# Order of the second mixers: products written between the steps of a recurrence

## The chip, the cores and the metric

The kernel runs on one core of a Trainium2 chip. The metric is the time of one execution on the device in microseconds; lower is better. Five engines work side by side, each on a queue of its own in a fixed order: TensorE (PE in the profile; its weight loads are PEld), VectorE (DVE), ScalarE (ACT), GpSimd (POOL) and SyncE (SP), which issues the transfers.

## The reference, cut to what matters

Two networks of two layers each work on 512 positions of 1024 channels, the second on the output of the first. The change touches the mixer of the second network, which runs three mixers on slices of one projection and joins them:

```python
def hybrid_mixer(h, positions, w_in, ...):
    proj = h @ w_in
    aq, ak, av, bq, bf, bv, bg, cqkv, cg, cb, ca = jnp.split(proj, split_at, axis=-1)
    # A: attention in a window of 128
    aq = partial_rope(rmsnorm_2(aq, q_norm), positions)
    ak = partial_rope(rmsnorm_2(ak, k_norm), positions)
    out_a = sliding_window_attention(aq, ak, av, sinks)
    # B: gated linear recurrence (HGRN2)
    log_f = jnp.logaddexp(jnp.log(lb), jnp.log1p(-lb) + jax.nn.log_sigmoid(bf))
    o_b = hgrn2_chunked(bq, log_f, bv)
    out_b = rmsnorm_2(o_b, hgrn_norm) * jax.nn.silu(bg)
    # C: gated delta rule, on convolved queries, keys and values
    cq, ck, cv = jnp.split(jax.nn.silu(causal_depthwise_conv(cqkv, conv_w)), ...)
    o_c = gated_delta_chunked(l2norm(cq), l2norm(ck), cv, beta, g)
    out_c = rmsnorm_2(o_c, gdn_norm) * jax.nn.silu(cg)
    return jnp.concatenate([out_a, out_b, out_c], axis=-1) @ w_out
```

## The kernel before, in words

Activations are held channel by channel: eight tiles of 128 channels x 512 positions. Every projection is a product in three parts: weights and activations are each split into a rounded half and the rest, and three matmuls (high x high, high x low, low x high) add up in PSUM. `load` (line 391) fetches a weight tile on SyncE, ScalarE rounds it (L381) and VectorE takes the rest (L382).

There are two kinds of product. A feature-major one (`lin_f_steps`) gives a tile of 128 output channels x 512 positions from 24 matmuls (lines L406, L407, L408 of `mm3`); its result goes to a function `ev`. A token-major one (`lin_t_steps`) gives four blocks of 128 positions; it yields after each eighth of its inner dimension, that is after 12 matmuls (L475, L476, L477), and evacuates all four blocks at its end. Both take their PSUM banks under the tag `mm`, which has four.

`second_mixer` runs in this order. Four feature-major products (w[0:4]) give the recurrence's gates and queries. One token-major product (`win2_t0`, 512 wide) gives its values and output gate, and the first two steps of the recurrence `hgrn` are taken between its last steps. Then the rest of `hgrn` is written out: two pairs of heads woven together, 10 steps each. In each of eight levels of a pair GpSimd takes a difference (L1260), ScalarE two exponentials (L1261, L1262), VectorE scales queries and keys (L1264, L1265), TensorE multiplies them (L1273), and VectorE merges the result into an accumulator (L1277, L1279). The two last steps of a pair combine the chunks (L1288 to L1312) and apply the values (L1330). The recurrence's PSUM tiles go under the tag `mx`, four banks, two per step.

Behind the recurrence stand a token-major product of 392 columns (`win2_t1`: the attention's values, the delta rule's gate `cg` and its two small gates), the gain of `cg` on GpSimd (L1751), and five feature-major products (w[10:15]): four tiles of the attention's queries and one of its keys. Their evacuation `ev` scales them (L1721), squares them (L663) and sums the squares per head by small matmuls into the tile `st` (L1724). The attention `swa` then rotates the five tiles on VectorE (L1084 to L1087) and normalises, until it says "ready". Six more feature-major products follow (w[4:10]), each with a convolution on VectorE (L832 to L844). Last, the attention and the delta rule `gdn` are woven step by step.

The written order is not the order in the queues. A planner in the framework takes it as a priority: it goes through the program with estimated durations and gives each engine the first ready instruction in the written order, and it assigns the buffers of each tag on the way. The queues are fixed before the run.

Of the kernel before, what the change touches and what calls it, by code (L numbers as in the profile page):

```python
# [249 lines left out]
class Net:  # L250
# [1456 lines left out]
    def second_mixer(self, x, l):  # L1707
        nc, V, G = self.nc, self.nc.vector, self.nc.gpsimd
        keep = {}

        def ev(o, ps):
            if 4 <= o < 10:
                keep[o] = L.conv(ps, self.vec("conv_w2", l)[:, 4 * (o - 4):4 * (o - 4) + 4], 3, None)
                return
            t = keep[o] = L.t(name="u")
            if o < 4:
                nc.scalar.copy(t, ps)
                return
            if o == 10:
                keep["st"] = self.ps("mx")  # L1720
            nc.scalar.activation(out=t, in_=ps, func=AF.Copy, scale=self.vec("q_norm" if o < 14 else "k_norm", l))  # L1721
            sq, i = self.square(ps), o - 10
            for b in range(NB):
                nc.tensor.matmul(keep["st"][:, 10 * b + 2 * i:10 * b + 2 * i + 2], sq[:, b * P:(b + 1) * P], self.bd64[:, 0:65:64],  # L1724
                                 start=True, stop=True)

        bv, bg, cg = (self.big((P, NB, 256), name=n) for n in ("bv", "bg", "cg"))
        L = self.using("l")
        av = L.t((P, NB, P), name="av")
        ba = self.small((P, NB, 8), "gba", 2)  # L1730

        def gate(t, ps):

            nc.scalar.activation(out=t, in_=ps, func=AF.Tanh, scale=0.5)
            V.scalar_tensor_tensor(t, t, 1.0, ps, op0=ALU.add, op1=ALU.mult)

        def evt0(b, ps):
            nc.scalar.copy(bv[:, b, :], ps[:, 0:256])
            gate(bg[:, b, :], ps[:, 256:512])

        def evt1(b, ps):
            nc.scalar.copy(av[:, b, :], ps[:, 0:128])
            gate(cg[:, b, :], ps[:, 128:384])
            V.tensor_copy(ba[:, b, :], ps[:, 384:392])

        w = self.tiled("win2_f", l, KD)
        y_a, y_c, last = [], [], []

        def gains(t, n):
            t4 = t.rearrange("p a (b c) -> p (a b) c", b=4)  # L1750
            G.tensor_tensor(t4, t4, self.row(n, l).unsqueeze(1).to_broadcast([P, 16, 64]), op=ALU.mult)  # L1751

        self.lin_f(w[0:4], x, ev, wide=4)
        gh = self.using("m", "mx").hgrn([keep[2], keep[3]], [keep[0], keep[1]], bv, bg, l, last)
        for n, _ in enumerate(self.lin_t_steps(self.d["win2_t0"][l], x, 512, evt0)):
            if n + 1 in (7, 8):
                next(gh)
        for n, _ in enumerate(gh):
            if n == 2:
                gains(bg, "hgrn_norm")  # L1760
        self.lin_t(self.d["win2_t1"][l], x, 392, evt1)
        gains(cg, "gdn_norm")
        self.lin_f(w[10:15], x, lambda o, ps: ev(o + 10, ps))
        ga = self.using("l", "mx").swa([keep[o] for o in range(10, 14)], keep[14], keep["st"], av, l, self.tab2, y_a)
        while next(ga) != "ready":
            pass
        y_b = last[0]()
        self.lin_f(w[4:10], x, lambda o, ps: ev(o + 4, ps))
        gc = self.using("m", "mm").gdn([keep[o] for o in range(4, 10)], cg, ba, l, y_c)
        drain(weave(gc, ga))  # L1770
        return y_a + y_b + y_c
# [49 lines left out]
def weave(*gens):  # L1821

    gens = list(gens)
    while gens:
        for g in list(gens):
            try:
                new = next(g)
            except StopIteration:
                gens.remove(g)
            else:  # L1830
                if new is not None:
                    gens.append(new)
                yield


def drain(gen):
    for _ in gen:
        pass
# [25 lines left out]
```

## Time and profile before

| | us |
|---|---|
| median of 3 runs | 3588.67 |
| lowest and highest | 3587.6, 3591.35 |
| the profiled execution | 3586.55 |
| its span, first to last instruction | 3584.7 |
| TensorE busy in the span | 3484.3 |
| VectorE busy | 1989.1 |
| ScalarE busy | 1364.5 |

The second network's mixers lie between 2100 and 2500 us (layer 0) and between 2840 and 3240 us (layer 1) of the span. A row of the timeline gives start, duration, engine, line, operation, the tiles written and read, their shapes and a count; in brackets stands how long the engine had been idle and what released it. A matmul's duration holds its run through the array, so neighbours overlap: a slot is the distance of two starts. PEclk is the granted TensorE clock as a share of 2.4 GHz.

### The profile page before, as it was taken

The numbers are of one execution on the slowest core, as the hardware profiler recorded it, in microseconds if no ns is written. First come the engines' busy times: TensorE is split into PE (matmuls) and PEld (weight loads), VectorE is DVE, ScalarE is ACT, GpSimd is POOL, SyncE is SP. The second block draws the span as 40 slices with busy tenths as digits, with TensorE's granted clock in tenths as the row PEclk, the third lists the DMA queues.
The fourth block names the chain that finished last, engine by engine and source line by source line (L and its number), as shares of the span: only waits on it lengthen the run. The fifth ranks groups of instructions, "written<-read, shape, count | busy, mean of one in ns | idle before, by whom it ended". The sixth has DMA issues, their size and how long they took to land.

```text
span 3584.7 us, 44503 instructions
## 1 busy us (share of the span) xinstructions
PE 3484.3 (97%) x17694; PEld 2901.8 (81%) x17694; DVE 1989.1 (55%) x3074; ACT 1364.5 (38%) x2231; POOL 140.5 (4%) x130
## 2 busy tenths in 40 slices
PE   9999999999999999999999998899999989999999
PEld 7888777888888888777888887788888877888887
DVE  6555665554665555674556577756333475654333
ACT  4223454323333223463223364354222453543221
POOL 0000000000000000000000003100000021000000
PEclk9999999999999999999999999899999999999999
DMA  5444212444334443202444321102333222022332
GB/s 167 141 135 129 84 32 68 142 145 128 127 100 142 146 138 100 91 15 95 146 148 137 94 77 54 62 7 75 108 98 101 78 71 68 1 71 90 100 99 83
DMA packets 114272, 349.06 MB, mean 97 GB/s; under 512 B 11536, under 2 KB 27920, under 8 KB 114064
## 3 DMA queue, kind: packets, MB, share of 16 engines
q1 hardware_dynamic: 114064, 346.21, 30.8%
q8 instruction: 140, 2.29, 0.3%
q14 instruction: 68, 0.56, 0.0%
HBM read 339.87 MB, written 2.10 MB: 95 GB/s over the span
## 4 chain that ended last, share of the span: by engine, by line
PE 87%; DVE 6%; issue 3%; ACT 2%; POOL 1%; DMA 1%; SPq 0%; POOLq 0%; DVEq 0%; ACTq 0%
PE mm L406 24%; PE mm L408 24%; PE mm L407 24%; PE mm L1481 1%; PE mm L1476 1%; PE mm L476 1%; PE mm L477 1%; PE mm L475 1%; PE mx L968 1%; DVE hacc L1279 1%; DVE wlo L382 1%; PE mm L809 1%; PE mx L948 1%; ACT sc L1138 1%; PE mx L1121 1%
## 5 line engine op out<-in xcount | busy, mean ns | idle before, releaser
L381 ACT CAST whi<-wraw 128x1024 fp32r<-128x1024 f32 (+3 forms) x540 | 553.4, 1029 | 1553.6 <-PE mm L407 1271.7
L406 PE MATMUL mm<-xh,whi 128*128 128x512 f32 (+1 forms) x2784 | 1053.3, 380 | 9.7 <-ACT whi L381 6.4
L407 PE MATMUL mm<-xl,whi 128*128 128x512 f32 (+1 forms) x2784 | 1055.8, 380 | 1.6 <-DVE xl L588 1.4
L408 PE MATMUL mm<-xh,wlo 128*128 128x512 f32 (+1 forms) x2784 | 1055.8, 380 | 0.3 <-DVE wlo L382 0.3
L382 DVE TENSOR_TENSOR wlo<-wraw,whi 128x1024 fp32r<-128x1024 f32 (+3 forms) x540 | 643.7, 1194 | 274.9 <-ACT whi L381 234.3
L406 PEld LDWEIGHTS mm<-xh,whi 128*128 128x128 f32 x2784 | 522.4, 189 | 107.8 <-ACT whi L381 6.4
L407 PEld LDWEIGHTS mm<-xl,whi 128*128 128x128 f32 x2784 | 524.9, 189 | 100.3 <-DVE xl L588 2.5
L408 PEld LDWEIGHTS mm<-xh,wlo 128*128 128x128 f32 x2784 | 524.8, 189 | 100.4 <-DVE wlo L382 3.1
L408 PE MATMUL mm<-hi,wlo 128*128 128x512 f32 (+1 forms) x1390 | 532.2, 383 | 2.1 <-DVE wlo L382 2.1
L406 PE MATMUL mm<-hi,whi 128*128 128x512 f32 (+1 forms) x1390 | 532.5, 384 | 0.2
L407 PE MATMUL mm<-lo,whi 128*128 128x512 f32 (+1 forms) x1390 | 531.8, 383 | 0.0
L408 PEld LDWEIGHTS mm<-hi,wlo 128*128 128x128 f32 x1390 | 261.3, 188 | 54.2 <-DVE wlo L382 4.2
L406 PEld LDWEIGHTS mm<-hi,whi 128*128 128x128 f32 x1390 | 261.1, 188 | 51.4 <-ACT hi L399 1.1
L407 PEld LDWEIGHTS mm<-lo,whi 128*128 128x128 f32 x1390 | 261.3, 188 | 50.3
L658 DVE SCALAR_TENSOR_TENSOR h<-mm,h 128x512 f32<-128x512 f32 x112 | 77.2, 691 | 224.2 <-PE mm L408 224.1
L1589 DVE SCALAR_TENSOR_TENSOR ada<-wraw,cond,ada 128x1024 f32<-128x1024 f32 x84 | 107.9, 1284 | 95.6 <-DMA wraw<-in_ada_w_dram 95.2
L637 DVE TENSOR_TENSOR gl<-mm,rstd 128x512 f32<-128x512 f32 x88 | 60.7, 690 | 155.1 <-PE mm L408 155.1
L636 DVE TENSOR_TENSOR silu<-mm,rstd 128x512 f32<-128x512 f32 x88 | 60.7, 689 | 145.2 <-PE mm L408 145.2
L658 DVE SCALAR_TENSOR_TENSOR h<-mm,mod,h 128x512 f32<-128x512 f32 (+1 forms) x70 | 48.9, 704 | 148.7 <-PE mm L408 148.7
L399 ACT CAST hi<-gl 128x512 fp32r<-128x512 f32 x132 | 82.2, 623 | 100.6 <-DVE gl L639 99.9
L633 DVE TENSOR_TENSOR gl<-silu,mm 128x512 f32<-128x512 f32 x44 | 30.2, 687 | 135.8 <-PE mm L408 135.8
L400 DVE TENSOR_TENSOR lo<-gl,hi 128x512 fp32r<-128x512 f32 x132 | 90.5, 686 | 15.4 <-ACT hi L399 15.4
(493 smaller groups left out, 3606.2 us busy)
## 6 DMA issues: line engine op xcount, KB each, us to landing
wraw<-in_ffn_gate_dram SPq DMA_DIRECT2D x130, 512.0 KB, 3.5
wraw<-in_ffn_up_dram SPq DMA_DIRECT2D x130, 512.0 KB, 4.0
wraw<-in_ada_w_dram SPq DMA_DIRECT2D x96, 512.0 KB, 3.7
wraw<-in_ffn_down_dram SPq DMA_DIRECT2D x96, 448.0 KB, 3.3
wraw<-in_win_f_dram SPq DMA_DIRECT2D x50, 512.0 KB, 3.5
wraw<-in_ffn_down_dram SPq DMA_DIRECT2D x48, 512.0 KB, 3.5
wraw<-in_w_out_dram SPq DMA_DIRECT2D x32, 512.0 KB, 3.5
wraw<-in_win_t_dram SPq DMA_DIRECT2D x16, 512.0 KB, 3.5
```

The lines of the kernel that those rows point to most:

```text
L381: self.nc.scalar.copy(hi[:, s], raw)
L382: self.nc.vector.tensor_tensor(lo[:, s], raw, hi[:, s].bitcast(F32), op=ALU.subtract)
L399: self.nc.scalar.copy(hi, src)
L400: self.nc.vector.tensor_tensor(lo, src, hi.bitcast(F32), op=ALU.subtract)
L406: T.matmul(ps, whi, xhi, start=first, stop=False)
L407: T.matmul(ps, whi, xlo, start=False, stop=False)
L408: T.matmul(ps, wlo, xhi, start=False, stop=last)
L475: T.matmul(ps, xh[:, bs], w[0][:, s], start=k == 0, stop=False)
L636: nc.vector.tensor_tensor(sg, gate_ps, rb, op=ALU.mult)
L637: nc.vector.tensor_tensor(gg, up_ps, rb, op=ALU.mult)
L658: self.nc.vector.scalar_tensor_tensor(h, ps[:, c], scale, h, op0=ALU.mult, op1=ALU.add)
L1589: V.scalar_tensor_tensor(acc, raw, cond[:, k:k + 1], acc, op0=ALU.mult, op1=ALU.add)
```

## The change

The tile `st` is taken under the tag `mm`. The products that stood behind the recurrence become a generator, of which one step is taken ahead of the rest of each loop pass over the recurrence's steps: eight passes with an eighth of the token-major product each, then the evacuation, the gain and the five feature-major products, one in every second pass. What is left when the recurrence ends is written behind it.

```diff
             if o == 10:
-                keep["st"] = self.ps("mx")
+                keep["st"] = self.ps("mm")
...
+        def others():
+            yield from self.lin_t_steps(self.d["win2_t1"][l], x, 392, evt1)
+            gains(cg, "gdn_norm")
+            for _ in self.lin_f_steps(w[10:15], x, lambda o, ps: ev(o + 10, ps)):
+                yield
+                yield
+
+        fill = others()
         for n, _ in enumerate(gh):
+            next(fill, None)
             if n == 2:
                 gains(bg, "hgrn_norm")
-        self.lin_t(self.d["win2_t1"][l], x, 392, evt1)
-        gains(cg, "gdn_norm")
-        self.lin_f(w[10:15], x, lambda o, ps: ev(o + 10, ps))
+        drain(fill)
```

## Rows read from the trace of the kernel before

**Rows 1.** The page, busy time of each engine, its share of the span and instructions.

```profile
PE 3484.3 (97%) x17694; PEld 2901.8 (81%) x17694; DVE 1989.1 (55%) x3074; ACT 1364.5 (38%) x2231; POOL 140.5 (4%) x130
```

**Rows 2.** Windows, layer 0: length, then busy time by engine, clock, DMA share.

```profile
core 0: us, PE busy (x) PEld busy (x) DVE busy (x) ACT busy (x) POOL busy (x), PEclk, DMA share, GB/s
2157.00:2217.00 60.00, 50.19 (x413) 41.41 (x411) 56.76 (x88) 24.76 (x62) 26.87 (x20) 1.00 0.14 45
2217.00:2228.00 11.00, 10.85 (x98) 10.33 (x98) 2.55 (x10) 4.15 (x8) 1.60 (x1) 1.00 0.14 47
2228.00:2256.00 28.00, 27.40 (x141) 22.07 (x140) 10.49 (x17) 10.18 (x15) 3.68 (x4) 1.00 0.24 80
2256.00:2288.00 32.00, 31.28 (x144) 26.08 (x145) 27.27 (x49) 11.43 (x17) 5.63 (x2) 1.00 0.26 82
2288.00:2326.00 38.00, 28.42 (x161) 24.36 (x161) 30.45 (x75) 15.88 (x39) 6.54 (x3) 0.73 0.10 32
```

**Rows 3.** Windows, layer 1, the stretch that answers to the last one.

```profile
3026.00:3064.00 38.00, 28.11 (x161) 24.04 (x161) 30.45 (x75) 16.01 (x40) 6.54 (x3) 0.73 0.10 31
```

**Rows 4.** Groups of TensorE, 2157 to 2217 us: count, busy and mean, idle before.

```profile
L475 PE MATMUL mm<-whi,xh 128*128 128x392 f32 x32 | 11.2, 352 | 0.0
...
L406 PE MATMUL mm<-xh,whi 128*128 128x512 f32 x14 | 5.9, 424 | 0.0
L407 PE MATMUL mm<-xl,whi 128*128 128x512 f32 x13 | 5.4, 418 | 0.0
```

**Rows 5.** Waits of TensorE, 2157 to 2326 us: in total, times, longest.

```profile
PE mx L1273 <- DVE hk L1265: 8.0, 12, 2.6
...
PE mx L1273 <- DVE hacc L1279: 1.0, 1, 1.0
```

**Rows 6.** Timeline of TensorE in the recurrence of layer 0.

```profile
2162.88 1.16 PE L1273 MATMUL mx<-hq,hk 64*128 64x128 f32 x16 [2.55 <-DVE hk L1265]
...
2167.37 1.16 PE L1273 MATMUL mx<-hq,hk 64*128 64x128 f32 x16
...
2186.54 1.16 PE L1273 MATMUL mx<-hq,hk 64*128 64x128 f32 x16 [1.09 <-DVE hk L1265]
2187.63 0.44 PE L475 MATMUL mm<-whi,xh 128*128 128x392 f32 x1
```

**Rows 7.** Timeline of TensorE among the products, two starts 24 matmuls apart.

```profile
2262.02 0.39 PE L406 MATMUL mm<-xh,whi 128*128 128x512 f32 x1
...
2267.46 0.39 PE L406 MATMUL mm<-xh,whi 128*128 128x512 f32 x1
```

**Rows 8.** Groups of VectorE, 2157 to 2326 us: two of the rotations' four operations.

```profile
L1084 DVE STREAM_SHUFFLE ro<-u 128x512 f32<-128x512 f32 x5 | 3.7, 736 | 0.0
L1085 DVE TENSOR_TENSOR ro<-ro,sin 128x512 f32<-128x512 f32 x5 | 3.5, 699 | 0.0
```

**Rows 9.** Timelines of ScalarE, VectorE and TensorE: queries, rotations, last product, last convolution.

```profile
2211.29 0.68 ACT L1721 ACTIVATE u<-mm,vecs 128x512 f32<-128x512 f32 x1
...
2251.98 0.59 ACT L663 ACTIVATE sq<-mm 128x512 f32<-128x512 f32 x1
...
2252.68 0.72 DVE L1084 STREAM_SHUFFLE ro<-u 128x512 f32<-128x512 f32 x1
...
2286.96 0.40 PE L408 MATMUL mm<-xh,wlo 128*128 128x512 f32 x1
...
2308.19 0.68 DVE L844 SCALAR_TENSOR_TENSOR cout<-cout,cacc 128x512 f32<-128x512 f32 x1
```

**Rows 10.** Timelines of GpSimd and VectorE at the recurrence's end.

```profile
2203.45 3.42 POOL L1751 TENSOR_TENSOR cg<-cg,rows 128x1024 f32<-128x1024 f32 x1 [3.27 <-DVE gba L1744]
...
2203.89 0.75 DVE L1265 TENSOR_TENSOR hk<-kt,he 128x512 f32<-128x512 f32 x1
...
2205.74 1.68 DVE L1288 TENSOR_TENSOR hx<-hl 128x512 f32<-128x512 f32 x1
...
2212.76 2.34 DVE L382 TENSOR_TENSOR wlo<-wraw,whi 128x1024 fp32r<-128x1024 f32 x2
```

**Rows 11.** ScalarE: its waits in 2157 to 2217 us, and one among the products.

```profile
ACT av L1742 <- PE mm L477: 4.6, 2, 2.5
...
2237.30 1.05 ACT L381 CAST whi<-wraw 128x1024 fp32r<-128x1024 f32 x1 [4.47 <-PE mm L407]
```

## The prediction

> **What bounds the kernel now.** I read the engine line of the page first [rows 1]: TensorE is busy 97% of the span, VectorE 55%, so in the mean nothing can be won beside TensorE. A mean hides stages, though, and the change touches only the mixers of the second block, 2157 to 2326 us in layer 0 and 2895 to 3064 us in layer 1. The busy times of their stretches come next [rows 2]: 60 us of recurrence, 11 us in which it closes, 28 us of products, 32 us of products with convolutions, 38 us in which the attention and the delta rule begin. In layer 1 the last stretch repeats with the same VectorE time and clock [rows 3], so I work out one layer and double it.
>
> The reader is to see two limits that take turns. In the recurrence VectorE is busy 56.76 of 60 us: it sets the pace, 3.5 us for each of 16 steps. In the 28 us of products TensorE is busy 27.40 and VectorE 10.49. In the last 38 us both have gaps, and the granted clock is 0.73: part of it ran at the lower level, 1.2 GHz, after TensorE had waited. A stage bound by VectorE next to one that VectorE sleeps through is what mixing could pay for.
>
> How much is mixed already? These products stand behind the recurrence in the program, yet many of their matmuls run in it: the TensorE groups of the first stretch [rows 4] hold all 96 matmuls of the token-major product (32 on each of three lines) and 40 of the 120 of the five feature-major ones (14, 13 and 13 on three lines). So the planner that orders the queues has filled gaps by itself, and the plain sum (44 us of products hidden) is wrong by a third and more.
>
> What is left are TensorE's waits [rows 5]: recurrence matmuls waited 8.0 us for the scaled keys on VectorE and 1.0 us for the accumulator. The timeline [rows 6] shows one: 1.09 us at L1273, and the next token-major matmul starts only behind it. The queue follows the plan, and VectorE ran later than the plan had it.
>
> **The change part by part.** No instruction is removed, added or reshaped. What moves is the place in the written order, the planner's priority.
>
> (a) *Filling the recurrence.* Each of the first eight recurrence steps is now followed by 12 token-major matmuls, later every second step by a product of 24. A 512-wide matmul takes a slot of 0.2267 us (24 of them from 2262.02 to 2267.46) [rows 7]; 18 of the 392-wide kind stood between two steps, so (4.49 - 1.16) / 18 = 0.185 us each [rows 6]. TensorE owes 96 x 0.185 = 17.8, 120 x 0.2267 = 27.2 and 16 steps of 1.16 = 18.6 us, 63.6 us in all, and the recurrence lasts 60. The two nearly balance, the best case for weaving. The gain is the waits that get filled, between 0 and 9.0 us [rows 5]. I take 8, near the upper end: at the priority of the neighbouring step the plan spreads the products evenly, where it now spends 18 narrow matmuls between early steps and has few left between later ones.
>
> (b) *Queries and keys arrive earlier.* VectorE owes the attention five rotations, each a shuffle of 0.736 and three operations of about 0.69 us, 2.8 us, 14.0 us together [rows 8]. They begin at 2252.68, right behind the last square for the normalisation on ScalarE (2251.98), although the first query tile was evacuated by 2211.97 [rows 9]. From 2217 to 2256 VectorE worked only 13.0 of 39 us [rows 2]. If the five products end with the recurrence, the rotations fall into that hole, and the six convolutions no longer queue behind them: the last one now ends at 2308.87, 21.5 us after its product's last matmul (2287.36) [rows 9]. More than the rotations' own time can't come back: between 0 and 14.0 us. I take 9: four of the five rotations, 11.2 us, lie in the 32 us stretch in which VectorE was full (27.27 us) and pushed that much into the next, but the delta rule's chain there has waits of its own (VectorE 30.45 of 38 us).
>
> (c) *What it costs.* The recurrence is VectorE's stretch, so new tenants cost there. Two of the five weight splits, a pair of 2.34 us, ran behind its last level (2212.76) [rows 10] and move in. The gate's gain on GpSimd (3.42 us) moves from behind the recurrence's own GpSimd steps to among them; while it ran, a VectorE operation took 0.75 us and one 1.68 [rows 10], where the usual is 0.69 [rows 8]: some 1.1 us. I count 3 us, between 0 and 3.5, as part of this was paid before.
>
> Of that GpSimd operation the Trainium skill says more ("SBUF — State Buffer", section "SBUF: two separate sides"): VectorE with two SBUF inputs and GpSimd hold a shared port exclusively for a whole instruction. By that rule the loss would be up to all of the 3.42 us, and the sum about 5 us less over both layers. The row of 0.75 us lies wholly beneath the GpSimd operation, so the trace doesn't bear the lock out here.
>
> (d) *Nothing, with cover.* The products' loads go past only the recurrence's mask loads on SyncE, issued before them in both kernels; the DMA share of the stretch is 0.14 [rows 2], so 0; a late load would delay its own product alone. The statistics' accumulator takes a PSUM bank from the products' tag in place of the recurrence's: three banks are left for products that use two at a time, so 0; uncovered, it costs a product one evacuation of 0.68 us [rows 9], 3.4 us a layer. The clock: 28.42 us at 0.73 would be 20.7 at 2.4 GHz, so 0 to 7.7 us; I take 0, since the waits that lower it belong to the delta rule's chain, and half, 3.9, in the best case.
>
> Sum per layer: 8 + 9 - 3 = 14 us, 28 us for both. The profiled execution took 3586.55 us (span 3584.7 and 1.85 around it), so 3558.6; the median of the runs shown is 2.1 us higher, hence 3561.
>
> **The rivals.** *Already woven.* The planner fills gaps whatever the written order, and that order decides only when two instructions are ready at once. Then (a) and (b) come to 0 to 4 us and (c) takes them back: 3582 to 3595. For it: 136 of 216 matmuls had moved already. Against it: the products' last square is still 35 us behind the recurrence's stretch.
>
> *The recurrence is held up (slower).* A recurrence matmul may now stand behind a whole product, 24 x 0.2267 = 5.4 us, while VectorE has one more step, 3.5 us, to do meanwhile; ScalarE's evacuation of that product would wait in front of the recurrence's exponentials too, as ScalarE waited 4.47 us for a product's matmul among the dense ones [rows 11]. If nothing overlaps, five products lengthen the recurrence by 27.2 us, and only the 80 matmuls now outside leave their place, 18.1 us: 9.1 us lost per layer, 3607 us. It decides from 4.6 us a step on (3.5 + 18.1 / 16). For it: with 18 narrow matmuls between them two steps did lie 4.49 us apart (2162.88, 2167.37) [rows 6]. Against it: a product comes every second step only, and ScalarE's waits of up to 2.5 us for token-major matmuls [rows 11] fell in a stretch in which VectorE was 95% busy.
>
> *All of it.* (a) 9.0, (b) 14.0, the clock 3.9, (c) 0: 26.9 us a layer, 3535.
>
> **How the numbers follow.** Forecast 0.49 (3545 to 3577); more than that, down to 3535, 0.12; already woven 0.19; held up 0.20. A difference under 0.2%, 7 us, is about what a measurement of this kernel can't tell from none. So faster 0.61, same 0.19, slower 0.20. The range runs from all of it, 3535, to cost (c) without a gain, 3588.7 + 7 = 3596; most of the slower rival lies beyond, and little below.
>
> **What would show it.** Right: the last square of the keys lies near 2230 instead of 2251.98; L1273's waits for keys fall from 8.0 to about 2 us; the first rotation starts before 2235; the last convolution ends within 12 us of its product. Wrong: if the recurrence's last accumulator step, now about 2212, comes 20 us later, it is held up; if the products end where they did, nothing was woven. If the products move but the rotations don't, only (a) is paid, 10 us in all. I would be wrong altogether if the chain of the delta rule, from the convolved keys on, sets the end and starts no earlier.

## The result, and the profile after

The changed kernel takes 3612.19 us, the median of 4 runs (3611.3 to 3618.83), against 3588.99 us for the kernel before beside it: 1.0073 times as long, with a 95% interval of 1.006 to 1.0085. (A ratio here is the record's estimate from all the times of the two kernels, not the quotient of the medians, which would be 1.0065.) It lies above the predicted 3561 us and outside the range of 3535 to 3596. The profiled execution has a span of 3609.5 us, 24.8 more than before. One of the 11 executions of before_dep_ro, further down, took 5808.8 us at a granted clock of 0.555, and its ratio leaves that one out.

The page's engine line, which answers to [rows 1]:

```profile
PE 3500.7 (97%) x17694; PEld 2916.5 (81%) x17694; DVE 1994.6 (55%) x3074; ACT 1364.7 (38%) x2231; POOL 141.6 (4%) x130
```

The same instructions, the same shares: this line shows nothing of the loss. The windows do. First the stretches of [rows 2], last the one of layer 1 in which it closes its second recurrence:

```profile
2157.00:2217.00 60.00, 49.41 (x350) 42.76 (x349) 48.97 (x75) 26.15 (x62) 26.75 (x20) 0.94 0.17 63
2217.00:2228.00 11.00, 10.32 (x80) 8.40 (x79) 5.56 (x10) 4.05 (x6) 0.00 (x0) 1.00 0.15 48
2228.00:2256.00 28.00, 26.17 (x186) 21.66 (x183) 15.12 (x27) 10.47 (x20) 4.95 (x2) 1.00 0.19 62
2256.00:2288.00 32.00, 27.55 (x138) 23.24 (x138) 23.47 (x41) 9.57 (x15) 6.74 (x3) 0.89 0.17 48
2288.00:2326.00 38.00, 31.24 (x170) 26.09 (x169) 27.09 (x58) 10.59 (x21) 6.54 (x3) 0.96 0.21 61
2994.00:3026.00 32.00, 27.68 (x137) 24.92 (x136) 17.77 (x36) 7.95 (x14) 11.67 (x4) 0.63 0.06 17
```

The reader is to see that VectorE does less in the recurrence (48.97 us where it did 56.76) and that TensorE, which was full at 1.00 from 2217 to 2288, now has gaps there and in part a lower clock (0.89). The one gain is the last stretch, 0.96 where it was 0.73. The layers don't lose alike. Their first recurrence matmuls start 2.82 us (2162.88 in [rows 6]) and 9.58 us later than before; the first row below is of before, the next fence of after:

```profile
2899.44 1.44 PE L1273 MATMUL mx<-hq,hk 64*128 64x128 f32 x10 [2.56 <-DVE hk L1265]
```

```profile
2165.70 1.16 PE L1273 MATMUL mx<-hq,hk 64*128 64x128 f32 x16 [2.54 <-DVE hk L1265]
...
2909.02 1.23 PE L1273 MATMUL mx<-hq,hk 64*128 64x128 f32 x8 [2.54 <-DVE hk L1265]
```

So 2.8 us of the 24.8 were there before anything moved (TensorE's queue is the same up to that point), 6.8 come in layer 0 and 15.2 in layer 1. The list of TensorE's waits from 2157 to 2326 us shows what is new in layer 0; it answers to [rows 5]:

```profile
PE mx L1273 <- DVE hk L1265: 6.2, 7, 2.5
PE mm L713 <- DVE ho L1335: 4.5, 2, 3.8
PE mx L1273 <- DVE gb L1354: 4.4, 1, 4.4
...
PE mm L1724 <- ACT sq L663: 2.5, 4, 0.7
```

The waits for keys shrank from 8.0 to 6.2 us, and 4.4, 4.5 and 2.5 us are new. TensorE's timeline shows the two large ones, GpSimd's what lies behind them:

```profile
2206.43 0.76 PE L1273 MATMUL mx<-hq,hk 64*128 64x128 f32 x2 [4.36 <-DVE gb L1354]
2207.12 1.86 PE L1724 MATMUL mm<-base,sq 128*128 128x2 f32 x8
2208.92 2.07 PE L1273 MATMUL mx<-hq,hk 64*128 64x128 f32 x14
...
2265.99 1.12 PE L713 MATMUL mm<-base,ho 128*128 128x128 f32 x4 [3.81 <-DVE ho L1335]
```

```profile
2197.70 4.57 POOL L1751 TENSOR_TENSOR cg<-cg,rows 128x1024 f32<-128x1024 f32 x1 [4.94 <-DVE gba L1744]
2202.22 3.52 POOL L1260 TENSOR_TENSOR he<-hl 128x512 f32<-128x512 f32 x3
...
2251.05 7.67 POOL L1080 TENSOR_TENSOR srn<-sms,nhalf 128x8 f32<-128x8 f32 x2 [38.93 <-DVE sms L1077]
2258.73 2.01 POOL L669 TENSOR_TENSOR pw<-hms,nhalf 128x8 f32<-128x8 f32 x1
```

The gain of `cg`, which stood behind all differences of the recurrence (the last of them began at 2198.74, the gain at 2203.45 [rows 10]), now stands ahead of four of them; three that VectorE, ScalarE and TensorE need next queue directly behind it. The 14 small matmuls after the wait take 2.07 us where 16 took 1.16 [rows 6]: they run at the lower clock. VectorE's timeline, with the recurrence's last accumulator step, the first rotation and the last convolution:

```profile
2204.15 0.69 DVE L1264 TENSOR_TENSOR hq<-u,he 128x512 f32<-128x512 f32 x1 [4.11 <-POOL he L1260]
...
2239.12 1.33 DVE L1279 COPY_PREDICATED hacc<-mats,mx 128x512 f32<-128x512 int32 x2
...
2249.74 0.72 DVE L1084 STREAM_SHUFFLE ro<-u 128x512 f32<-128x512 f32 x1
...
2314.93 0.68 DVE L844 SCALAR_TENSOR_TENSOR cout<-cout,cacc 128x512 f32<-128x512 f32 x1
```

### The profile page after: what moved, and what is told of

Its sections match the earlier page's. It is cut to its first block, busy times and chain, and to the rows that moved or that the text cites. A ratio compares the mean times of both kernels' runs of the same rounds, so it can differ in the third digit from the quotient of the medians.

```text
span 3609.5 us, 44483 instructions
## 1 busy us (share of the span) xinstructions
PE 3500.7 (97%) x17694; PEld 2916.5 (81%) x17694; DVE 1994.6 (55%) x3074; ACT 1364.7 (38%) x2231; POOL 141.6 (4%) x130
## 5 line engine op out<-in xcount | busy, mean ns | idle before, releaser
L400 DVE TENSOR_TENSOR lo<-gl,hi 128x512 fp32r<-128x512 f32 x132 | 90.5, 685 | 15.2 <-ACT hi L399 15.1
```

The lines of the kernel that those rows point to most:

```text
L400: self.nc.vector.tensor_tensor(lo, src, hi.bitcast(F32), op=ALU.subtract)
```

## Experiments

Each line gives the median and the ratio to the kernel before, timed beside it, with the 95% interval. A difference of 0.001 in the ratio is 3.6 us. The kernels were timed in several rounds, so most of them meet only through the kernel before; a difference of two ratios is uncertain by some 0.0015, 5 us. "Tied" means that an instruction gets one more input, so that it can't start before another has ended; "covering products" are matmuls written where TensorE would else wait for the recurrence's end.

| kernel | us | ratio | interval |
|---|---|---|---|
| changed | 3612.19 | 1.0073 | 1.0060 to 1.0085 |
| t1_only: token-major part alone | 3609.21 | 1.0054 | 1.0042 to 1.0066 |
| t1_dep: the same, gain tied | 3596.26 | 1.0016 | 1.0007 to 1.0025 |
| two_dep: and two products in halves | 3588.58 | 1.0000 | 0.9990 to 1.0009 |
| gain_late: changed, gain written last | 3616.93 | 1.0071 | 1.0058 to 1.0084 |
| gain_dep: changed, gain tied | 3602.55 | 1.0034 | 1.0017 to 1.0051 |
| gain_dep_again | 3598.43 | 1.0028 | 1.0016 to 1.0039 |
| gain_srn_dep: and the power tied | 3607.74 | 1.0058 | 1.0045 to 1.0071 |
| halves: changed, products in halves | 3615.07 | 1.0073 | 1.0060 to 1.0086 |
| halves_dep: and gain tied | 3597.88 | 1.0025 | 1.0016 to 1.0034 |
| cover2: changed, two covering products | 3604.50 | 1.0035 | 1.0022 to 1.0047 |
| dep_cover2: and gain tied | 3588.15 | 1.0004 | 0.9994 to 1.0014 |
| halves_dep_cover2: and in halves | 3590.02 | 0.9995 | 0.9985 to 1.0005 |
| dep_cover2_ro: blocks, rotations' own tag | 3591.41 | 1.0007 | 0.9998 to 1.0016 |
| hdc2_ro: halves, rotations' own tag | 3576.97 | 0.9973 | 0.9960 to 0.9986 |
| hdc2_ro_again | 3579.20 | 0.9976 | 0.9968 to 0.9985 |
| before_ro: unwoven, rotations' own tag | 3583.34 | 0.9985 | 0.9976 to 0.9995 |
| before_dep_ro: and gain tied | 3580.15 | 0.9974 | 0.9965 to 0.9983 |
| conv_first: unwoven, groups exchanged | 3594.10 | 1.0021 | 1.0012 to 1.0031 |

### First four: one part at a time

The first theory was the prediction's slower rival: whole products, 24 matmuls, hold the recurrence up. Rivals were the gain on GpSimd, the PSUM bank, and the end of the recurrence without cover.

The token-major part alone (t1_only):

```diff
         def others():
             yield from self.lin_t_steps(self.d["win2_t1"][l], x, 392, evt1)
-            gains(cg, "gdn_norm")
-            for _ in self.lin_f_steps(w[10:15], x, lambda o, ps: ev(o + 10, ps)):
...
         drain(fill)
+        gains(cg, "gdn_norm")
+        self.lin_f(w[10:15], x, lambda o, ps: ev(o + 10, ps))
```

> One part of the change alone: the token-major product stays written between the recurrence's steps and the statistics tile stays under the products' PSUM tag, but the gain of cg and the five feature-major products stand behind the recurrence again. Theory (the recurrence is held up by whole products of 24 matmuls written in front of its steps): without them nothing is held up, 3584 to 3594 us, last accumulator step of layer 0 between 2209 and 2216, TensorE's queue as before up to the first of the five products. Rival (the PSUM bank of the statistics tile, or the token-major part, costs the time): 3600 us or more.

1.0054: the theory fell. TensorE's queue is as before until the products, none of these is written between the steps, and three quarters of the loss are there. Its trace, TensorE, GpSimd and VectorE:

```profile
2199.75 1.16 PE L1273 MATMUL mx<-hq,hk 64*128 64x128 f32 x16
...
2207.07 2.08 PE L1273 MATMUL mx<-hq,hk 64*128 64x128 f32 x16 [5.49 <-DVE hk L1265]
```

```profile
2198.36 4.55 POOL L1751 TENSOR_TENSOR cg<-cg,rows 128x1024 f32<-128x1024 f32 x1 [4.93 <-DVE gba L1744]
2202.87 3.50 POOL L1260 TENSOR_TENSOR he<-hl 128x512 f32<-128x512 f32 x3
```

```profile
2198.28 0.67 DVE L1264 TENSOR_TENSOR hq<-u,he 128x512 f32<-128x512 f32 x1
2198.88 0.68 DVE L1265 TENSOR_TENSOR hk<-kt,he 128x512 f32<-128x512 f32 x1
2199.48 1.21 DVE L382 TENSOR_TENSOR wlo<-wraw,whi 128x1024 fp32r<-128x1024 f32 x1
2204.78 0.69 DVE L1264 TENSOR_TENSOR hq<-u,he 128x512 f32<-128x512 f32 x1 [4.09 <-POOL he L1260]
```

The gain is written behind the loop here, and stands ahead of four differences all the same. What moved it, as I read the queues, are the evacuations: at their new priority VectorE does them early (the last ends at 2198.35, before at 2203.44), so in the plan the gain is probably ready at a moment when GpSimd is free, and takes it. No run tested this by itself. The wait of 5.49 us and 0.92 for slow matmuls (2.08 - 1.16) are 6.4 us in one layer.

The gain written behind the loop in the changed kernel (gain_late):

```diff
             yield from self.lin_t_steps(self.d["win2_t1"][l], x, 392, evt1)
-            gains(cg, "gdn_norm")
...
         drain(fill)
+        gains(cg, "gdn_norm")
```

> The changed kernel with the GpSimd gain of cg written behind the loop again, all else as changed. Theory (whole products hold the recurrence up): the gain is only the 4.36 us for which TensorE waited once in each layer, part of which comes back as another wait: 3603 to 3612 us, last accumulator step of layer 0 at 2234 to 2240. Rival (the gain on GpSimd, in front of three differences of the recurrence, is what throws it back): 3588 to 3597 us, last accumulator step before 2222.

1.0071, and it tells nothing on the gain: the queues of TensorE, VectorE, ScalarE and GpSimd hold the same instructions in the same order as in the changed kernel, so this is a repeat of it. The place in the text did not move the instruction, and another means was needed (below).

Halves (halves):

```diff
-            for _ in self.lin_f_steps(w[10:15], x, lambda o, ps: ev(o + 10, ps)):
-                yield
+            for o, (src, nt) in enumerate(w[10:15]):
+                wt, ps = self.load(src, KD * P), self.ps("mm")
+                for k in range(KD):
+                    if k == KD // 2:
+                        yield
+                    s = slice(k * P, (k + 1) * P)
+                    self.mm3(ps, (wt[0][:, s], wt[1][:, s]), x[k], k == 0, k == KD - 1)
+                ev(o + 10, ps)
                 yield
```

> The changed kernel with each of the five products written in two halves of 12 matmuls, one half in front of every recurrence step in place of a whole product in front of every second; the evacuation behind the second half, the gain of cg where the change put it. Theory (blocks of 24 matmuls, 5.4 us, are longer than VectorE's 3.5 us a step): two thirds or more of the loss comes back, 3590 to 3600 us, last accumulator step of layer 0 near 2225. Rival one (the gain on GpSimd): it is still there, 3606 to 3614. Rival two (the end of the recurrence has lost the products that covered it, whatever their size): 3606 to 3614, with 4 us or more of waits of the transposes at L713.

1.0073, the same as the changed kernel. Both its rivals are left.

Two covering products (cover2):

```diff
         drain(fill)
+        self.lin_f(w[4:6], x, lambda o, ps: ev(o + 4, ps))
...
         y_b = last[0]()
-        self.lin_f(w[4:10], x, lambda o, ps: ev(o + 4, ps))
+        self.lin_f(w[6:10], x, lambda o, ps: ev(o + 6, ps))
```

> The changed kernel with two of the six products with convolutions written ahead of the rotations and of the recurrence's last transposes, so that TensorE has 48 matmuls (10.9 us) to do while the recurrence closes. Theory (whole products hold the recurrence up): the late end stays, only the 4.5 us of waits at L713 and the slow clock behind them go, 3599 to 3609 us. Rival (the loss is the uncovered end of the recurrence): 3586 to 3596 us.

1.0035: half of the loss (13.6 us by the ratios) is bought by 48 matmuls in the place where the recurrence closes. The time lies in the first theory's range and the late end stays (the last accumulator step ends at 2239.45), so this run by itself doesn't rule that theory out.

### The gain, tied behind the recurrence

To move the gain on GpSimd alone, its row gets a zero added that the last pair makes out of L1299's result; it then can't start before that. All other queues keep their order but for these tiny operations (t1_dep, gain_dep, halves_dep, halves_dep_cover2).

```diff
             V.tensor_scalar(kn, e[:, 0:P], dec[:, 1, :], None, op0=ALU.mult)
+            self.zero = self.small((P, 1), "gzero", 2)
+            V.tensor_scalar(self.zero, kn[:, 0:1], 0.0, None, op0=ALU.mult)
...
+        row = self.small((P, 64), "grow", 2)
+        V.tensor_scalar(row, self.row("gdn_norm", l), rec.zero, None, op0=ALU.add)
+        cg4 = cg.rearrange("p a (b c) -> p (a b) c", b=4)
+        G.tensor_tensor(cg4, cg4, row.unsqueeze(1).to_broadcast([P, 16, 64]), op=ALU.mult)
```

> The kernel with the token-major part alone, and the gain of cg tied to the recurrence: its row gets a zero added that comes from the last pair's L1299, so it stands behind all differences on GpSimd, as before the change, instead of ahead of the last four; the queue of the matmuls is the same as without that tie. New theory (the gain ahead of four differences makes TensorE wait 5.49 us once, and the matmuls behind that wait run at the lower clock): nearly all of the 20 us comes back, 3586 to 3594 us, longest wait of L1273 under 3 us, clock 1.00 from 2200 to 2225 us. Rival (the PSUM bank of the statistics, or the delta rule's small gates with their table loads among the exponentials): 3600 to 3610 us.

1.0016 against 1.0054: 13.6 us, the price of the gain's place (8 to 19 us by the two intervals), close to 12.8 (twice 6.4). GpSimd's row and TensorE's longest wait:

```profile
2222.05 2.36 POOL L1775 TENSOR_TENSOR cg<-cg,grow 128x1024 f32<-128x1024 f32 x1 [21.76 <-DVE grow L1773]
```

```profile
PE mx L1273 <- DVE hk L1265: 7.6, 9, 2.6
```

The expected 3586 to 3594 was missed by 2 us: some 6 us of the token-major part remain. Its ScalarE shows one candidate: the delta rule's small gates now run among the recurrence's exponentials, with a table load on either side where before only one was due (the second row is the exponential's):

```profile
2203.41 1.28 ACT L853 ACT_TABLE_LOAD   x1
2204.70 0.31 ACT L853 ACTIVATE gla<-gla,one 128x16 f32<-128x16 f32 x1
2205.03 1.28 ACT L1261 ACT_TABLE_LOAD   x1
```

That is argued, not shown: no run took them out, and two_dep, below, has such loads too and loses nothing.

> The changed kernel with the gain of cg tied behind the recurrence in the same way, the five products woven as whole blocks of 24 as changed. New theory (gain and slow clock cost 8 to 10 us a layer): 3592 to 3602 us; what is left over 3590 is the price of the blocks and of the uncovered end. Old theory (blocks of 24 alone hold the recurrence up): 3606 to 3613 us, last accumulator step of layer 0 still past 2234.

1.0034, and 1.0028 in the repeat below: 14 to 16 us of the changed kernel's loss are the gain's place. The rest is not. The time is the new theory's, within a microsecond; but the mark of the old one is there too, as the last accumulator step ends at 2235.16, still past 2234. The blocks do make the recurrence late; what that costs is tested with dep_cover2, below.

> The same with the products in halves of 12 in front of every step. If blocks of 24 cost something beside the gain, this lies 4 us or more below the kernel with whole blocks and the tied gain, and the last accumulator step of layer 0 near 2222; if size doesn't matter, the two are equal within 3 us. If the uncovered end of the recurrence costs (4.5 us of waits at L713 and slow matmuls behind), it stays above 3592.

1.0025, within the intervals of the whole blocks. The list of TensorE's waits in this kernel, longest first, starts with the recurrence's end:

```profile
PE mm L713 <- DVE ho L1337: 7.5, 2, 4.5
PE mx L1273 <- DVE hk L1265: 6.3, 7, 2.5
```

> The same again with two of the six products with convolutions written ahead of the rotations and the transposes at L713. If gain, block size and uncovered end are all that went wrong, then what was promised for the filled waits and the earlier queries is left: 3570 to 3586 us. Rival (VectorE, with rotations and convolutions side by side, is late with the delta rule anyway): 3587 to 3596 us.

0.9995: with tied gain, cover and halves the loss is gone, and nothing is won. The time is that of the rival (VectorE late anyway), whose mechanism was not followed in the trace. In layer 0 a wait now stands behind the cover; layer 1 has none of this length:

```profile
2280.52 0.82 PE L676 MATMUL mx<-base,sp 128*128 128x128 f32 x4 [4.45 <-ACT sp L682]
```

### What the earlier queries are worth, and the cover

The rotated tiles share the tag `sq` with the squares, so the first rotation gets its buffer behind the last square, whatever the order of the products. One line gives them a tag that is free there (before_ro from the kernel before, hdc2_ro from halves_dep_cover2):

```diff
-            r = self.t(name="ro", tag="sq")
+            r = self.t(name="ro", tag="ns")
```

> The kernel before with the rotated tiles under another SBUF tag (three buffers that stand free there) in place of the tag they share with the squares; no order is changed. It prices the step of earlier queries by itself. If the rotations waited for the squares' buffers and their 14 us of VectorE stood in the way of the convolutions, the first rotation falls to about 2230 us, the last convolution from 2308.9 to 2300 or earlier and the time to 3570 to 3582 us. If the convolutions are bound by their products, not by VectorE, the rotations move and the time stays, 3584 to 3592 us.

The first rotation moves by 34 us (from 2252.68 [rows 9]), the last convolution ends at 2306.64 instead of 2308.87, and the time falls to 0.9985, some 5 us for both layers. That is between the two guesses: the rotations moved, and the convolutions and the time gained less than the first guess had it.

```profile
2218.72 0.73 DVE L1084 STREAM_SHUFFLE ro<-u 128x512 f32<-128x512 f32 x1
...
2305.96 0.68 DVE L844 SCALAR_TENSOR_TENSOR cout<-cout,cacc 128x512 f32<-128x512 f32 x1
```

> The kernel with halves, tied gain and two covering products, and the rotated tiles under the same other tag. If the products' move was to pay through earlier rotations and only the buffers held these back, 3572 to 3584 us with the first rotation before 2225 us; if VectorE's place for the rotations does not matter, equal to the kernel without it within 4 us (3586 to 3594).

0.9973, below the kernel without the other tag (0.9995); its interval overlaps that of before_ro (0.9985). The first rotation begins at 2209.00. Whether the weaving has a part in it is the question further down.

Only two products woven, three left as cover (two_dep; halves and tied gain as above):

```diff
-            for o, (src, nt) in enumerate(w[10:15]):
+            for o, (src, nt) in enumerate(w[10:12]):
...
         drain(fill)
...
+        self.lin_f(w[12:15], x, lambda o, ps: ev(o + 12, ps))
```

> Only the first two of the five products woven, in halves, the other three behind the recurrence as its cover, and the gain of cg tied behind it. If the uncovered end is what is left of the loss with halves and tied gain (1.0025 of before), no wait of 4 us at L713 and 3583 to 3592 us; if it is the weaving as such, 3594 to 3600 us.

1.0000, and no wait for `ho` is left at L713: the products that stay behind are cover enough. (Three products fewer are woven too, which this run doesn't part from the cover.) Products of its own cover the recurrence's end as well as borrowed ones do.

A try at another order, from the unwoven kernel (conv_first):

```diff
         gains(cg, "gdn_norm")
+        self.lin_f(w[4:10], x, lambda o, ps: ev(o + 4, ps))
         self.lin_f(w[10:15], x, lambda o, ps: ev(o + 10, ps))
...
         y_b = last[0]()
-        self.lin_f(w[4:10], x, lambda o, ps: ev(o + 4, ps))
```

> The kernel before with its two groups of products exchanged: the six with convolutions first, then the five of queries and keys, nothing woven. VectorE is busy 13 of 39 us behind the recurrence and 27 of 32 in the stretch that follows; with the convolutions (some 4.4 us each) in the empty stretch and the rotations behind, both halves fit. If VectorE's late convolutions set the start of the delta rule, 3565 to 3582 us; if the attention's scores, now late by 15 us of rotations, take their place, 3585 to 3605 us.

1.0021: slower. The second guess, the attention taking the place of the delta rule, fits the time; it was not followed in the trace.

### Does the weaving itself pay, and does the block's size matter?

> The kernel before with the two mends that need no weaving: the gain of cg tied behind the recurrence and the rotated tiles under the other tag. If the weaving itself is worth nothing, this equals the woven kernel with all mends within 3 us (3576 to 3584); if the products woven into the recurrence pay by themselves, as the prediction's first term had it, this lies 5 us or more above it (3582 to 3588).

> The woven kernel with all mends (halves, tied gain, two covering products, rotated tiles under the other tag) once more, beside the unwoven one: 3574 to 3582 us if it repeats; within 3 us of the unwoven one if the weaving is worth nothing, 5 us or more below it if it pays.

0.9974 unwoven and 0.9976 woven, side by side, with interval ends 4 us away at most: the weaving, with its two covering products, is worth nothing that shows.

> The changed kernel with whole blocks of 24, the gain of cg tied behind the recurrence and two covering products. Against the same with halves (0.9995 of before) it prices the block's size alone: within 3 us of it if size doesn't matter (3586 to 3593), 3596 us or more if blocks of 24 hold the recurrence up by themselves.

1.0004 against 0.9995 in halves: 3 us, inside the intervals.

> The same with the rotated tiles under the other tag. If the block's size doesn't matter, 3574 to 3582 us, as with halves; if it does, 5 us or more above them.

1.0007 against 0.9976: here blocks cost 11 us. The profiled runs of the two in the same stretches, first blocks, then halves:

```profile
2220.00:2251.00 31.00, 29.17 (x183) 24.01 (x182) 18.70 (x34) 10.75 (x19) 7.47 (x3) 0.89 0.16 52
2251.00:2270.00 19.00, 19.00 (x84) 17.54 (x84) 5.04 (x11) 3.66 (x6) 5.61 (x3) 0.64 0.00 0
```

```profile
2220.00:2251.00 31.00, 29.50 (x206) 24.26 (x205) 19.07 (x40) 15.26 (x26) 4.87 (x3) 1.00 0.15 52
2251.00:2270.00 19.00, 19.00 (x100) 16.20 (x100) 11.15 (x20) 6.31 (x10) 8.20 (x3) 1.00 0.10 28
```

TensorE is busy in both, but at 0.64 with blocks. Halves are not free of this, though. hdc2_ro and hdc2_ro_again are one kernel, and the profiled run of the first (3585.78 us, the other 3575.43) has these rows, of layer 0 and of the same place in layer 1:

```profile
2251.00:2270.00 19.00, 19.00 (x79) 17.03 (x79) 7.14 (x14) 3.97 (x6) 10.65 (x4) 0.64 0.01 4
2989.00:3008.00 19.00, 19.00 (x123) 17.13 (x123) 9.47 (x19) 4.53 (x8) 10.66 (x4) 1.00 0.09 28
```

In its layer 0 the last convolution ends 145.9 us behind the start of the recurrence's first matmul, in its layer 1 137.0, and in layer 0 of hdc2_ro_again 137.2. So a fall of the clock in this stretch goes with some 9 us in a layer, with the same instructions in the same order. It came in both layers with blocks (0.64, and 0.57 in layer 1), in one and in none with halves. The 11 us may be no more than that; a price of the block's size is not shown. Why the clock fell is open: in the profiled runs of hdc2_ro and dep_cover2_ro TensorE had no wait of 1 us from 2196 us up to the fall in layer 0.

Last, the recurrence's end: is it the missing cover, or that the attention's power (L1080, 7.67 us) now goes ahead of the recurrence's (L669) on GpSimd? The power is tied behind it with the same zero trick (gain_srn_dep, where `rec.tie` is made from L669's result), beside gain_dep once more:

```diff
         V.tensor_scalar(rs_, st[:, 0:40], 1.0 / 64, EPS, op0=ALU.mult, op1=ALU.add)
+        V.tensor_scalar(rs_, rs_, self.tie, None, op0=ALU.add)
```

> The changed kernel with the gain of cg tied behind the recurrence, once more, as the neighbour of the next run: 1.0025 to 1.0045 of before.

> The same with the attention's power of its statistics (L1080, 7.66 us on GpSimd) tied behind the recurrence's second power (L669), so that the order of the two is as before the change. If that order makes the 3.8 us wait of the transposes at L713, the wait falls under 1 us and the time 6 us or more below its neighbour, 3588 to 3597 us; if the end of the recurrence has simply lost the products that covered it, a wait of some 6 us stands there all the same and the two are equal within 4 us, 3597 to 3604.

1.0058, not faster but slower. With the old order on GpSimd the wait stands there all the same (four small matmuls, L676, moved behind it), and in the profiled run the whole stretch is at half the clock, 1.2 GHz. Its row at L713, and its window:

```profile
2265.25 1.12 PE L713 MATMUL mm<-base,ho 128*128 128x128 f32 x4 [4.76 <-DVE ho L1340]
```

```profile
2251.00:2270.00 19.00, 13.31 (x58) 12.00 (x58) 10.22 (x23) 4.01 (x7) 8.59 (x4) 0.50 0.00 0
```

So the order on GpSimd does not make the wait, and of the two guesses the missing cover is left. Behind the recurrence TensorE was busy for 10.85 of 11 and 27.40 of 28 us before [rows 2], and here for 13.31 of 19.

## Why the prediction was wrong, step by step

**What bounds.** The reading of two limits that take turns was right, but it left out what the stretch of 28 us does beside its own work: the products that fill TensorE there (27.40 us) also cover the recurrence's closing chain, from its last accumulator to the transposes at L713. I read it as a place to empty. Emptied, it cost 9 to 14 us for both layers (1.0028 and 1.0034 to 1.0004 with tied gain, 1.0073 to 1.0035 without).

**(a) Filling the recurrence, +8 a layer.** Wrong, by all of its size. The waits for keys went from 8.0 to 6.2 us, not to 2, and with every obstacle that was found out of the way the weaving is worth nothing that shows (0.9976 woven, 0.9974 not). The reason stood among the rivals: for the token-major product the planner had filled the gaps, and TensorE's queue stayed the same to the matmul up to the first of the five others. (The 44 us of products are 45.0 by the text's own terms, 17.8 + 27.2, and 26.9 of them ran in the recurrence already; nothing rests on it.) For the rest, a wait that was filled in the recurrence came back where the filling had been taken from.

**(b) Queries and keys earlier, +9 a layer.** Wrong twice. The first rotation came at 2249.74, not before 2235, since its buffer stands behind the last square under the tag `sq`, and the squares come with the products, which ended only 2.9 us earlier (last square 2251.98 [rows 9], now the first row):

```profile
2249.04 0.59 ACT L663 ACTIVATE sq<-mm 128x512 f32<-128x512 f32 x1
```

```profile
2301.14 0.40 PE L408 MATMUL mm<-xh,wlo 128*128 128x512 f32 x1
```

I looked at when the query was there and not at whose buffers the rotation needs. The convolutions do follow their products more closely, as foretold (the last one ends at 2315.61, 14.1 us after their last matmul, the second row, where it was 21.5), but behind products that end later. And the term itself was mis-sized: with the rotations in the hole, it is some 5 us for both layers, not 18 (before_ro).

**(c) The gain, -3 a layer.** This is the step that failed most. I priced the gain by what VectorE loses while it runs, 1.1 us, and did not ask what queues behind it on GpSimd: four of the recurrence's differences. That is 13.6 us for both layers (1.0054 to 1.0016), and 14 to 16 in the changed kernel. The text even named the place ("to among them").

The trace does bear out, after all, what the Trainium skill says in "SBUF — State Buffer", section "SBUF: two separate sides": whoever starts first holds the shared port for its whole instruction. In t1_only VectorE is the holder. The lone gain takes 2.36 us (t1_dep); the one at 2198.36 begins beside a chain of VectorE operations with two SBUF inputs that ends at 2200.69 (2199.48 + 1.21), and from there to the next difference at 2202.87 are 2.18 us. The row of 0.75 us beneath the gain, which I took as a proof against the rule [rows 10], only shows that the gain was waiting. VectorE's rows of before on either side of it:

```profile
2203.30 0.75 DVE L1264 TENSOR_TENSOR hq<-u,he 128x512 f32<-128x512 f32 x1
...
2204.50 1.41 DVE L1279 COPY_PREDICATED hacc<-mats,mx 128x512 f32<-128x512 int32 x2
```

The chain had begun 0.15 us ahead of the gain, and from the start of the first operation that reads PSUM (2204.50) to the gain's end at 2206.87 (2203.45 + 3.42) are 2.37 us, the length of the lone gain. The operation of 1.68 us (0.67 alone, at 2215.03) is the one that was kept out, until about that end. So the lock can explain 2.2 us of the wait of 5.5, by which the gain is longer; the rest is its place.

**(d) Nothing for DMA, bank and clock.** The bank: right, two_dep has it and is at 1.0000. The clock: wrong. I saw it as something to win in the last 38 us, and it was won there (0.73 to 0.96), but the lower clock came into stretches that had run at 1.00. In layer 0 (0.94 and 0.89) it did so with the new waits of 4.36 and 3.81 us. In layer 1 (0.63) it fell 15 us ahead of the wait at L713, while TensorE was busy:

```profile
3001.00:3016.00 15.00, 15.00 (x73) 14.76 (x72) 4.96 (x11) 2.92 (x5) 7.48 (x2) 0.51 0.00 0
```

What takes 15 us at half the clock would take about 7.5 at the full one. By this estimate, from the row alone, the clock is most of the 8.4 us that layer 1 lost beyond layer 0 (15.2 less 6.8).

**The rivals.** "Held up" came true in sign and nearly in size (3607), and its mark too: the last accumulator step ended at 2240.45 (2239.12 + 1.33), and was over by 2212.76 before [rows 10]: 28 us, 25 beyond the late start. That the size came near is luck, since the loss is made of the gain's place and the missing cover, which the rival did not have. Its mechanism was only half right. Blocks in front of the recurrence's steps do make it late, but lateness alone costs nothing that shows: with tied gain and cover (dep_cover2) whole blocks are at 1.0004, and the last accumulator step is still this late:

```profile
2231.75 1.33 DVE L1279 COPY_PREDICATED hacc<-mats,mx 128x512 f32<-128x512 int32 x2
```

"Already woven" was right about why nothing was to be won. I had given the two 0.39 together; the missing rival was the gain's place.

**What remains open:** the 6 us of t1_dep, and why the clock falls behind the woven recurrence in some layers and executions and not in others. The times of hdc2_ro lie in two groups (five from 3572.84 to 3576.97 us, four from 3583.47 to 3587.96), so a gain of the weaving that needs the full clock is not ruled out.

## What to carry to other kernels

Before work is moved to fill a wait, ask what it covers where it stands now; here, with the busiest engine at 97%, filling one hole opened the other. Price a moved instruction on its own queue first, by who stands behind it, even on an engine that is 4% busy; and where a planner orders the queues, look at the order it made, since a place in the text may move nothing (gain_late) or move something else. A buffer's tag decides when a step can start as much as its inputs do: of everything tried here, one tag and one tie in the unwoven kernel gave 0.26%, and the whole reordering on top of them nothing.

## What the runs showed of the hardware

An operation on GpSimd that lies over VectorE's was stretched from 2.36 to 4.55 us, while VectorE's own kept their 0.67 to 1.21 us (t1_only); where the gain held on, a VectorE operation of 0.67 us took 1.68 (before). After waits of 4.36 and 5.49 us TensorE's next matmuls ran at the lower of its two levels, 1.2 GHz: 16 small ones in 2.08 us instead of 1.16. After a wait of 2.55 us both occur: in t1_dep the 16 behind it took 2.08 us in layer 0, and 1.16 in layer 1 behind one of 2.56. The clock also fell with TensorE busy: 0.64 in a stretch of 19.00 of 19.00 us, where another execution of the same kernel had 1.00 throughout. What tells these apart is not shown by these runs.
